# Six more gate blocks as plain matmuls beside the attention, and fewer by seven products, in a decoder layer on one Trainium2 core

## The chip, the cores and the metric

The kernel runs on one core of one Trainium2 chip. The metric is the device time of one launch in microseconds. Engines are named as in the profile: PE is TensorE (PEld its weight loads), DVE VectorE, ACT ScalarE, POOL GpSimd, SP SyncE, which issues nearly all DMAs. SBUF is the on-chip memory, PSUM holds matmul results.

## The reference

One layer of a decoder for 1024 prompt rows and 32 sample rows (1056 columns, as everything is kept transposed), width 1024, all fp32:

```python
h = layer_norm(ALPHA * x + 0.5 * swiglu(x, f1_w1, f1_w3, f1_w2), ln1_g, ln1_b)
z = h @ w_in + b_in               # 42 blocks of 128: 18 for q, k, v; 4 u; 4 v of the spatial gate; 8 ga; 8 gb
# q, k, v: dilated window attention, 3 groups x 4 heads, softmax; groups combined by their denominators
att = combine_groups(outs, lses)
zz = gelu(uv); u, vr = zz[..., :SGU_W], zz[..., SGU_W:]
yb = u * mixed(layer_norm(vr))    # chunks of 128 rows, lower triangular weights
mix = (sigmoid(ga) * (att @ w_oa) + sigmoid(gb) * (yb @ w_ob)) @ w_out
h = layer_norm(ALPHA * h + mix, ln2_g, ln2_b)
h = layer_norm(ALPHA * h + 0.5 * swiglu(h, f2_w1, f2_w3, f2_w2), ln3_g, ln3_b)
```

## The kernel before

Each fp32 matmul is made of three fp32r matmuls (`mm3`, L224): activations and weights are split into a rounded high part (a cast on ACT, L235) and a low part (a subtraction on DVE, L236). The 1056 columns are four chunks of 264.

The stages are `ffn` (first half step), `widen` (the projection z), `mix` (attention, spatial gate, gated products, output projection) and `ffn` again. `widen` computes a block of z in one of two ways. **Plain** (`gate8`): 24 matmuls of 128x128 by 264 columns per chunk, 96 per block; a weight unit is loaded and split (`unit`), ACT evicts with bias and function into a tile M, and a DMA stores it to `zD`. **By seven products** (`pair`): two blocks at once by a Strassen-like scheme, 7 x 24 = 168 matmuls for two, with sums of weights made by `prep` (casts on ACT, sums on POOL, subtractions on DVE). `SPLIT` lists the blocks by seven products in order, `DENSE` the plain ones: 6 at the start (`NLEAD`), the first `CHUNKED` of them chunk by chunk as the normalized chunks come, and `NTAIL` in `mix`.

In `mix` the normalized activations are kept (16 slots) for the last gate blocks. Attention and spatial gate are Python generators in three queues (`bg`, `mid`, `slow`): after each chunk of matmuls `tick(n, m)` runs n steps of `bg`, m of `slow` and 3 of `mid`. `attend(i)` is one of six attention units (head pair, group); L1145 are its scores, L1153 bias and minimum on DVE, L1157 the exponential on ACT, L1168 the transposes, L1184 the products with v, L1206 the last transpose of a unit. After three units `combine` makes the weights of the three groups (DMAs through `mlD` and `cD`), `sample` computes the 32 sample rows on DVE in slabs of keys. Then `local(n)` computes block n of yb @ w_ob, times its gate (`product`, L1491, which evicts the PSUM bank), and a last loop that of att @ w_oa. Bank tags are `mm` (3 buffers) and `ax` (5). SBUF tags are S (37 slots of 4.2 KB a partition), W (8), M (6), R and Q (2 each). A scheduler that simulates the program sets the order on each engine; each engine and each DMA queue then runs its own list in order.

Of the kernel before, what the change touches and what calls it, by code (L numbers as in the profile page):

```python
# [52 lines left out]
HPG = [(hp, g) for hp in range(2) for g in range(3)]  # L53
PAIRS = [HPG[2 * i : 2 * i + 2] for i in range(3)]
URGENT = 300
STEPS = dict(lead=6, strassen=3, seven=2, out=2, tail=5, wob=2, wout=3)
PAUSE = 6
REST = 3
GAP = 4
# [7 lines left out]
QKV = [s * 6 + 2 * g + hp for hp, g in HPG for s in range(3)]  # L67
GATES = [*range(34, 42), *range(26, 34)]
NLEAD = 6
NTAIL = 4  # L70
CHUNKED = 2
SPLIT = [*QKV, 22, 23, 24, 25, 18, 19, 20, 21, *GATES[NLEAD : 16 - NTAIL]]
DENSE = GATES[:NLEAD] + GATES[16 - NTAIL :]
NZ = len(SPLIT) // 2


class Trunk:
# [848 lines left out]
                nc.vector.scalar_tensor_tensor(self.sbias[e, i], p[e], -1.0, mks[e, g], op0=ALU.mult, op1=ALU.add)  # L926
            yield

    def gate8(self, w, nb, c, *steps):
        nc = self.nc  # L930
        p = self.mm_tile()[:, :C]
        self.dense8(p, w, c)
        t = self.M([P, C])
        with self.urgent():
            nc.scalar.activation(t, p, AF.Sigmoid, bias=self.bin(nb))
        nc.sync.dma_start(self.zD[nb][:, c * C : c * C + C], t)
        self.tick(*steps)

# [19 lines left out]
    def pair(self, f, between):  # L958

        nc = self.nc  # L960
        n1, n2 = SPLIT[2 * f], SPLIT[2 * f + 1]
        one, two, three = self.banks()
        ta, tc = self.S([P, NT]), self.S([P, NT])
        gate = n1 >= 26

        def lin(t, nb):
            neg = nb < 6
            return t, nb, self.qb[:, nb : nb + 1] if neg else self.bin(nb), -0.125 if neg else 1.0

        def put(bank, y, e, fn=AF.Identity):  # L970
            t, nb, b, sc = y

            def act(x):
                for o, view in self.parts(t, nb, 2 * x + e):
                    nc.scalar.activation(o, view(bank[x]), fn, bias=b, scale=sc)  # L975
# [20 lines left out]
        def sig(t, x, o, n):  # L996
            c0 = (2 * x + o) * C
            nc.scalar.activation(t[:, c0 : c0 + n * C], t[:, c0 : c0 + n * C], AF.Sigmoid)

        a, c = lin(ta, n1), lin(tc, n2)  # L1000
        go(one, 1, True, put(one, a, 0))
        go(two, 2, True, add(two, a, 0), *([lambda x: sig(ta, x, 0, 1)] if gate else []))
# [3 lines left out]
        go(three, 4, False, add(three, c, 0), *([lambda x: sig(tc, x, 0, 2)] if gate else []))  # L1006
        self.send(tc, n2)
        go(one, 3, False, put(one, a, 1, AF.Sigmoid if gate else AF.Identity))
# [19 lines left out]
    def widen(self):  # L1028
# [22 lines left out]
        for c in range(NC):  # L1051
            self.drain(lns.pop(c))
            if c == NC - 1:
                self.slow.append(self.spread(1, Y, self.A, nc.vector))
            for n in range(CHUNKED):
                self.gate8(units[n], DENSE[n], c, STEPS["lead"], 1)
        units = Y = None
        for n in range(CHUNKED, NLEAD):
            w = self.unit(a["wzp"][n])
            if n == NLEAD - 1:  # L1060
                begin(0)
            for c in (1, 3, 0, 2):
                self.gate8(w, DENSE[n], c, STEPS["lead"], 1)
                if n == NLEAD - 1:
                    next(preps[0], None)
        self.A = None
# [32 lines left out]
    def attend(self, i):  # L1099
# [110 lines left out]
        nc.sync.dma_start(D_.rearrange("m h (i x) -> (m h i) x", x=P), mt)  # L1210
        yield
        if g == 2:
            self.slow.append(self.combine(hp))
            if hp:
                self.slow.append(self.sample_join())

    def combine(self, hp):
# [40 lines left out]
        yield  # L1258
        att = self.S([P, NT])
        self.att[hp] = att  # L1260
        cb = self.S([P, NP])
        for g in range(3):
            for h in range(2):
                nc.sync.dma_start(cb[64 * h : 64 * h + 64], self.cD[hp, g, h].partition_broadcast(64))
            yield
            yield
            aT = self.attT.pop((hp, g))
            if g == 0:
                nc.vector.tensor_tensor(att[:, :NP], aT, cb, op=ALU.mult)
            else:  # L1270
                nc.vector.tensor_tensor(aT, aT, cb, op=ALU.mult)
                nc.vector.tensor_tensor(att[:, :NP], att[:, :NP], aT, op=ALU.add)
            yield

    def sample_rows(self, *blocks):
        nc, a = self.nc, self.a
        yield
        p = self.ax_tile()[:NS, : 2 * P].rearrange("p (s x) -> p s x", s=2)
        for x, (_, t) in enumerate(blocks):
            nc.tensor.transpose(p[:, x], t[:, NP:], self.ident)  # L1280
# [100 lines left out]
    def sgu_norm(self):  # L1381
# [22 lines left out]
        self.swt, self.swb, self.ssb = wt, wb, sb  # L1404
        self.vr = [self.fetch_z(22 + i) for i in range(4)]
        yield from self.pause(4)
        for t in self.vr:
            nc.scalar.activation(t, t, AF.Gelu)
            yield
        vn = [self.S([P, 2, 512]) for _ in range(5)]  # L1410
        mv = self.X([P, 9, 2], "smv", 1)
        nc.vector.memset(mv, 1.0)
# [28 lines left out]
    def sgu_mix(self, gg):  # L1441
# [4 lines left out]
        self.yb[gg] = (hi, lo)  # L1446
        f = slice(gg * P, gg * P + P)
        g = self.cols[:, 90 + gg : 91 + gg]
        nc.scalar.activation(u, u, AF.Gelu)
        yield from self.pause(1)  # L1450
        for b in range(3):
            p = self.ax_tile()
            if b < 2:
# [20 lines left out]
    def mix(self):  # L1474
# [40 lines left out]
        self.drain()  # L1515
        split_att()
        done = 0

# [24 lines left out]
        self.bg.append(sums)  # L1543
        m2 = []
        for n in range(KB):
            wa, ta = self.unit(a["wo"][n], 2 * P), self.fetch_z(26 + n)
            if n < KB // 2:
                local(KB // 2 + n)
            for c in range(NC):
                product(wa, att, c, ta)  # L1550
                self.tick(2)
            nc.vector.tensor_tensor(mt[n], mt[n], ta, op=ALU.add)  # L1552
# [206 lines left out]
```

## Time and profile before

| what | value |
|---|---|
| median of 3 runs | 2310.39 us (2308.38 to 2310.87) |
| profiled execution | 2307.22 us, its span 2305.4 us |
| PE busy | 2164.4 us (94%) |
| DVE, ACT, POOL busy | 1576.9, 935.5, 339.0 us |
| mean granted TensorE clock | 0.964 |

Busy TensorE by slice of 57.6 us, in tenths, and the clock granted to it:

```profile
PE   9999999999998999999898864699999999999997
PEclk9999999999999999999997886899999999999999
```

Read from the left: `ffn` up to slice 12, then `widen` to slice 19, `mix` from slice 19 to 28, `ffn` again. Slices 20 to 25 are those in which TensorE is neither full nor at full clock.

### The profile page before, as it was taken

The numbers are of one execution on the slowest core, as the hardware profiler recorded it, in microseconds if no ns is written. First come the engines' busy times: TensorE is split into PE (matmuls) and PEld (weight loads), VectorE is DVE, ScalarE is ACT, GpSimd is POOL, SyncE is SP. The second block draws the span as 40 slices with busy tenths as digits, with TensorE's granted clock in tenths as the row PEclk, the third lists the DMA queues.
The fourth block names the chain that finished last, engine by engine and source line by source line (L and its number), as shares of the span: only waits on it lengthen the run. The fifth ranks groups of instructions, "written<-read, shape, count | busy, mean of one in ns | idle before, by whom it ended". The sixth has DMA issues, their size and how long they took to land. (4 is left out here: it accounts for less than half of the span.)

```text
span 2305.4 us, 43046 instructions
## 1 busy us (share of the span) xinstructions
PE 2164.4 (94%) x17209; PEld 2107.5 (91%) x17209; DVE 1576.9 (68%) x2722; ACT 935.5 (41%) x1713; POOL 339.0 (15%) x250
## 2 busy tenths in 40 slices
PE   9999999999998999999898864699999999999997
PEld 8999999999988999999876654699999999999997
DVE  8777767566788337878535465658777777746787
ACT  5444444311136333423388830226444344421124
POOL 0423323000000022232000000000323333200000
PEclk9999999999999999999997886899999999999999
DMA  4445454788753246665744334422355454596731
GB/s 159 140 149 187 154 182 168 262 315 295 296 175 117 80 162 218 204 227 196 265 148 137 105 115 134 174 112 96 129 177 180 159 181 158 186 347 253 274 141 76
DMA packets 161048, 416.83 MB, mean 181 GB/s; under 512 B 23808, under 2 KB 57328, under 8 KB 158160
## 3 DMA queue, kind: packets, MB, share of 16 engines
q1 hardware_dynamic: 160416, 413.55, 51.0%
q8 instruction: 135, 2.21, 0.4%
q14 instruction: 65, 0.53, 0.1%
q10 hardware_dynamic: 432, 0.54, 0.1%
HBM read 301.64 MB, written 158.57 MB: 200 GB/s over the span
## 5 line engine op out<-in xcount | busy, mean ns | idle before, releaser
L224 PE MATMUL ax<-S,W 128*128 128x264 f32 x5688 | 743.0, 284 | 0.6 <-ACT S L975 0.6
L224 PEld LDWEIGHTS ax<-S,W 128*128 128x128 f32 x5688 | 712.7, 188 | 2.3 <-ACT S L975 1.2
L224 PE MATMUL mm<-S,W 128*128 128x264 f32 x4632 | 638.7, 294 | 72.1 <-DVE S L1491 59.1
L224 PEld LDWEIGHTS mm<-S,W 128*128 128x128 f32 x4632 | 605.6, 196 | 84.8 <-DVE S L1491 61.2
L224 PE MATMUL ax<-S,S 128*128 128x264 f32 x3432 | 505.4, 285 | 0.5 <-DVE S L984 0.5
L224 PEld LDWEIGHTS ax<-S,S 128*128 128x128 f32 x3432 | 453.6, 188 | 1.9 <-DVE S L984 0.7
L224 PE MATMUL mm<-S,S 128*128 128x264 f32 x2472 | 390.8, 286 | 14.1 <-ACT S L235 9.5
L224 PEld LDWEIGHTS mm<-S,S 128*128 128x128 f32 x2472 | 337.3, 189 | 16.5 <-ACT S L235 10.0
L235 ACT CAST W<-R 128x1024 fp32r<-128x1024 f32 (+3 forms) x170 | 125.8, 756 | 427.0 <-PE mm L224 195.8
L366 POOL TENSOR_TENSOR Q<-R 128x512 f32<-128x512 f32 x53 | 73.8, 1392 | 847.2 <-DMA R<-w13a 237.4
L235 ACT CAST W<-Q 128x1024 fp32r<-128x1024 f32 (+1 forms) x82 | 80.9, 987 | 233.5 <-POOL Q L367 127.7
L236 DVE TENSOR_TENSOR W<-R,W 128x1024 fp32r<-128x1024 f32 (+3 forms) x170 | 148.1, 878 | 20.7 <-ACT W L235 20.6
L778 DVE SCALAR_TENSOR_TENSOR S<-ax,S 128x264 f32<-128x264 f32 x240 | 98.9, 426 | 58.0 <-PE ax L224 57.4
L441 DVE TENSOR_TENSOR S<-ax,M 128x264 f32<-128x264 f32 x84 | 33.5, 432 | 151.9 <-PE ax L224 151.9
L236 DVE TENSOR_TENSOR S<-Q,S 128x1024 fp32r<-128x1024 f32 (+2 forms) x90 | 127.7, 1419 | 7.1 <-ACT S L235 6.3
L235 ACT CAST S<-Q 128x1024 fp32r<-128x1024 f32 (+2 forms) x90 | 89.5, 994 | 100.6 <-PE ax L224 72.0
L103 POOL CAST S<-ones 128x1 fp32r<-128x1 f32 x32 | 13.5, 444 | 785.5 <-DVE S L1552 382.0
L236 DVE TENSOR_TENSOR W<-Q,W 128x1024 fp32r<-128x1024 f32 (+1 forms) x82 | 94.8, 1156 | 41.1 <-ACT W L235 41.0
L367 POOL TENSOR_TENSOR Q<-Q,R 128x512 f32<-128x512 f32 x53 | 87.6, 1652 | 2.7
L236 DVE TENSOR_TENSOR S<-S,M 128x528 fp32r<-128x528 f32 x72 | 85.3, 1185 | 2.5 <-ACT M L235 0.9
L374 POOL TENSOR_TENSOR Q<-R,Q 128x512 f32<-128x512 f32 x53 | 86.5, 1633 | 1.4
L372 POOL TENSOR_TENSOR Q<-R,R 128x512 f32<-128x512 f32 x53 | 80.7, 1523 | 20.7 <-ACT M L437 13.5
(200 smaller groups left out, 2089.2 us busy)
## 6 DMA issues: line engine op xcount, KB each, us to landing
ws<-st SPq DMA_DIRECT2D x144, 256.0 KB
S<-sumsA SPq DMA_DIRECT2D x63, 528.0 KB
S<-sumsB SPq DMA_DIRECT2D x63, 528.0 KB
M<-kv SPq DMA_DIRECT2D x96, 256.0 KB
sumsA<-M SPq DMA_DIRECT2D x90, 264.0 KB
sumsB<-M SPq DMA_DIRECT2D x90, 264.0 KB
R<-w13b SPq DMA_DIRECT2D x44, 512.0 KB
S<-zD SPq DMA_DIRECT2D x42, 528.0 KB
```

Source lines behind the costliest of these rows:

```text
L103: self.nc.gpsimd.tensor_copy(t[:, 0, :1] if len(shape) == 3 else t[:, :1], self.ones[:, :1])
L224: mm = lambda a, b, s, e: nc.tensor.matmul(o, a[:, cc], b, start=s, stop=e, skip_group_check=True)
L235: a = self.nc.scalar.copy(hi, src)
L236: b = self.nc.vector.tensor_tensor(lo, src, hi.bitcast(F32), op=ALU.subtract)
L366: tt(s12[:, lo], cd[:, lo], cd[:, hi], op=ALU.add)
L367: tt(s12[:, hi], s12[:, lo], ab[:, lo], op=ALU.subtract)
L372: tt(s34[:, lo], ab[:, lo], cd[:, lo], op=ALU.subtract)
L374: tt(s34[:, hi], ab[:, hi], s12[:, hi], op=ALU.subtract)
L441: go(one, 5, False, lambda x: tt(h[:, x, 1], one[x], p7[:, x], op=ALU.add))
L778: nc.vector.scalar_tensor_tensor(y(x, r, e), bank[x], HALF, y(x, r, e), op0=ALU.mult, op1=ALU.add)
```

## The change

- 26 instead of 32 blocks of z go by seven products (13 pairs instead of 16); the six are gates, and become plain blocks in `mix`: `NTAIL` is 10 instead of 4. The first six of the ten go block by block, the last four chunk by chunk. Per chunk 3 instead of 5 steps of `bg` run.
- Gates in `mix` are stored with bias but without Sigmoid; the Sigmoid is applied to the whole loaded block just before its products.
- The Gelu of u and v is applied in `pair` as the blocks are evicted, instead of after loading in the spatial gate.
- Loads of gates for the products stand two blocks ahead. `combine` runs in `mid` instead of `slow`, with three buffers for the group weights instead of one. `sample_rows` waits four steps instead of one.
- Three instead of two lead blocks go chunk by chunk (`CHUNKED`).

```diff
-STEPS = dict(lead=6, strassen=3, seven=2, out=2, tail=5, wob=2, wout=3)
+STEPS = dict(lead=6, strassen=3, seven=2, out=2, tail=3, wob=2, wout=3)
-NTAIL = 4
-CHUNKED = 2
+NTAIL = 10
+LAST = 4
+CHUNKED = 3
+LATE_GATES = DENSE[NLEAD:]
...
-    def gate8(self, w, nb, c, *steps):
+    def gate8(self, w, nb, c, fn, *steps):
...
-            nc.scalar.activation(t, p, AF.Sigmoid, bias=self.bin(nb))
+            nc.scalar.activation(t, p, fn, bias=self.bin(nb))
...
-        gate = n1 >= 26
+        fn = None if n1 < 18 else AF.Gelu if n1 < 26 else AF.Sigmoid
...
-            self.slow.append(self.combine(hp))
+            self.mid.append(self.combine(hp))
...
-        cb = self.S([P, NP])
-        for g in range(3):
+        cbs = [self.S([P, NP]) for _ in range(3)]
+        for g, cb in enumerate(cbs):
             for h in range(2):
                 nc.sync.dma_start(cb[64 * h : 64 * h + 64], self.cD[hp, g, h].partition_broadcast(64))
-            yield
-            yield
+        yield from self.pause(3)
+        for g, cb in enumerate(cbs):
             aT = self.attT.pop((hp, g))
...
-        yield
+        yield from self.pause(4)
         p = self.ax_tile()[:NS, : 2 * P].rearrange("p (s x) -> p s x", s=2)
...
-        for t in self.vr:
-            nc.scalar.activation(t, t, AF.Gelu)
-            yield
...
-        nc.scalar.activation(u, u, AF.Gelu)
-        yield from self.pause(1)
...
-            mt[n] = self.fetch_z(34 + n)
+            if n + 2 < KB:
+                mt[n + 2] = self.fetch_z(36 + n)
+            if 34 + n in LATE_GATES:
+                nc.scalar.activation(mt[n], mt[n], AF.Sigmoid)
...
-        units = [self.unit(a["wzp"][NLEAD + n]) for n in range(NTAIL)]
+        for n in range(NLEAD, NLEAD + NTAIL - LAST):
+            w = self.unit(a["wzp"][n])
+            for c in (0, 2, 1, 3):
+                self.gate8(w, DENSE[n], c, AF.Identity, STEPS["tail"], 1)
+        units = {n: self.unit(a["wzp"][n]) for n in range(NLEAD + NTAIL - LAST, NLEAD + NTAIL)}
         for c in range(NC):
-            for n in range(NTAIL):
-                self.gate8(units[n], DENSE[NLEAD + n], c, STEPS["tail"], 1)
+            for n in units:
+                self.gate8(units[n], DENSE[n], c, AF.Identity, STEPS["tail"], 1)
         units = self.A = None
+        for n in range(2):
+            mt[n] = self.fetch_z(34 + n)
...
-        self.drain()
+        ta = [self.fetch_z(26 + n) for n in range(2)]
+        while self.bg or self.mid or self.slow:
+            self.tick(1, 1)
...
-            wa, ta = self.unit(a["wo"][n], 2 * P), self.fetch_z(26 + n)
+            wa = self.unit(a["wo"][n], 2 * P)
+            if n + 2 < KB:
+                ta.append(self.fetch_z(28 + n))
             if n < KB // 2:
                 local(KB // 2 + n)
+            if 26 + n in LATE_GATES:
+                nc.scalar.activation(ta[n], ta[n], AF.Sigmoid)
             for c in range(NC):
-                product(wa, att, c, ta)
+                product(wa, att, c, ta[n])
```

Lines after L70 move by 2 to 13 in the changed kernel: L224 becomes L226, L935 L937, L1157 L1159, L1206 L1208, L1264 L1266, L1491 L1488.

How the lists of the engines change, at three places. First ACT at the start of `mix`, in the first attention unit. L935 (L937) is the eviction of a gate chunk, L1157 (L1159) the exponential, L1172 (L1174) the copy of transposed probabilities. Before:

```order
L1172 COPY S_13529<-ax_13521 128x2x128
L1172 COPY S_13529<-ax_13522 128x512
L935 ACTIVATE M_13777<-mm_13752,cols 128x264
L1157 ACT_TABLE_LOAD
L1157 ACTIVATE S_13532,X_13460<-S_13532,X_13460 128x256 x4
L935 ACT_TABLE_LOAD
L935 ACTIVATE M_13877<-mm_13852,cols 128x264
L1172 COPY S_13564<-ax_13554 128x512
L1172 COPY S_13564<-ax_13555 128x512
L1157 ACT_TABLE_LOAD
L1157 ACTIVATE S_13567,X_13460<-S_13567,X_13460 128x256 x4
```

Now:

```order
L1174 COPY S_12815<-ax_12808 128x512
L1159 ACTIVATE S_12818,X_12758<-S_12818,X_12758 128x256 x3
L937 ACTIVATE M_13103<-mm_13078,cols 128x264
L1174 COPY S_12850<-ax_12840 128x512
L1174 COPY S_12850<-ax_12841 128x512
L1159 ACTIVATE S_12853,X_12758<-S_12853,X_12758 128x256 x4
L937 ACTIVATE M_13172<-mm_13147,cols 128x264
```

The loads of a function table between exponential and gate eviction are gone.

Second PE, in an attention unit of the third group (before) and of the second group (now). L1145 (L1147) are scores, L1168 (L1170) transposes, L1184 (L1186) products with v, L224 (L226) with a tile mm a gate block. Before:

```order
L1184 MATMUL ax_14221<-S_14203,Q_14108 64x128 x4
L1168 MATMUL ax_14226<-ident,S_14206 128x128
L1168 MATMUL ax_14227<-ident,S_14206 128x128
L1145 MATMUL ax_14236<-S_13736,S_13734 128x128 x2
L1145 MATMUL ax_14237<-S_13736,S_13734 128x128 x2
L1168 MATMUL ax_14226<-ident,S_14206 128x128
L1168 MATMUL ax_14227<-ident,S_14206 128x128
L1184 MATMUL ax_14221<-S_14232,Q_14108 64x128 x4
```

Now:

```order
L1186 MATMUL ax_13327<-S_13342,Q_13181 64x128 x4
L226 MATMUL mm_13675<-S_8222,W_13581 128x264
L226 MATMUL mm_13675<-S_8224,W_13581 128x264
L226 MATMUL mm_13675<-S_8222,W_13582 128x264
L1170 MATMUL ax_13401<-ident,S_13345 128x128
L1170 MATMUL ax_13402<-ident,S_13345 128x128 x2
L1147 MATMUL ax_13413<-S_12694,S_12692 128x128
L1147 MATMUL ax_13413<-S_12694,S_12692 128x256
```

The last three of a gate chunk's 24 matmuls stand here between products and transposes, the other 21 ahead of the products; before, the units of the third group ran with none beside them.

Third SP, at the end of the attention. L1264 (L1266) loads the group weights, which L1257 (L1259) stored; L1083 (L1085) loads a block of z. S_14994 and S_15120 are the gates of `local(0)` and `local(1)` before, S_15320 and S_15322 now. Before:

```order
L1083 DMA S_14955<-zD 128x1056
L1083 DMA S_14994<-zD 128x1056
L1083 DMA S_15120<-zD 128x1056
L1357 DMA M_15528<-jD 64x66 x4
L1210 DMA mlD<-X_15075 32x128
L1117 DMA M_15078<-bD 64x64
```

Now:

```order
L938 DMA zD<-M_15313 128x264
L1359 DMA M_15366<-jD 64x66 x4
L209 DMA ws<-st 16x4096
L1259 DMA cD<-S_15109 16x128 x3
L1266 DMA S_15142<-cD 64x1024 x2
L1266 DMA S_15143<-cD 64x1024 x2
L1266 DMA S_15144<-cD 64x1024 x2
L1085 DMA S_15320<-zD 128x1056
L1085 DMA S_15322<-zD 128x1056
L1085 DMA S_15331<-zD 128x1056
```

The loads of the first gates stand behind the last weights' loads now; before they stood ahead of both head pairs' combinations.

More of the change, by code (lines that the diff above doesn't have):

```diff
@@ L994, in go, with bend @@
             between()
-        def sig(t, x, o, n):
+        def bend(t, x, o, n):
             c0 = (2 * x + o) * C
-            nc.scalar.activation(t[:, c0 : c0 + n * C], t[:, c0 : c0 + n * C], AF.Sigmoid)
+            nc.scalar.activation(t[:, c0 : c0 + n * C], t[:, c0 : c0 + n * C], fn)
         a, c = lin(ta, n1), lin(tc, n2)
         go(one, 1, True, put(one, a, 0))
-        go(two, 2, True, add(two, a, 0), *([lambda x: sig(ta, x, 0, 1)] if gate else []))
+        go(two, 2, True, add(two, a, 0), *([lambda x: bend(ta, x, 0, 1)] if fn else []))
         go(one, 6, False, put(one, c, 0))
@@ L1005, in pair @@
         go(one, 5, False, add(one, c, 1))
-        go(three, 4, False, add(three, c, 0), *([lambda x: sig(tc, x, 0, 2)] if gate else []))
+        go(three, 4, False, add(three, c, 0), *([lambda x: bend(tc, x, 0, 2)] if fn else []))
         self.send(tc, n2)
-        go(one, 3, False, put(one, a, 1, AF.Sigmoid if gate else AF.Identity))
+        go(one, 3, False, put(one, a, 1, fn or AF.Identity))
         self.send(ta, n1)
@@ L1055, in widen @@
             for n in range(CHUNKED):
-                self.gate8(units[n], DENSE[n], c, STEPS["lead"], 1)
+                self.gate8(units[n], DENSE[n], c, AF.Sigmoid, STEPS["lead"], 1)
         units = Y = None
@@ L1062, in widen @@
             for c in (1, 3, 0, 2):
-                self.gate8(w, DENSE[n], c, STEPS["lead"], 1)
+                self.gate8(w, DENSE[n], c, AF.Sigmoid, STEPS["lead"], 1)
                 if n == NLEAD - 1:
@@ L1545, in mix @@
         for n in range(KB):
-            wa, ta = self.unit(a["wo"][n], 2 * P), self.fetch_z(26 + n)
+            wa = self.unit(a["wo"][n], 2 * P)
+            if n + 2 < KB:
+                ta.append(self.fetch_z(28 + n))
             if n < KB // 2:
                 local(KB // 2 + n)
+            if 26 + n in LATE_GATES:
+                nc.scalar.activation(ta[n], ta[n], AF.Sigmoid)
             for c in range(NC):
-                product(wa, att, c, ta)
+                product(wa, att, c, ta[n])
                 self.tick(2)
-            nc.vector.tensor_tensor(mt[n], mt[n], ta, op=ALU.add)
+            nc.vector.tensor_tensor(mt[n], mt[n], ta[n], op=ALU.add)
             m2.append((self.S([P, NT], F32R), self.S([P, NT], F32R)))
```

## The prediction

> **What bounds the kernel now.** I read the times by stage first, to see where TensorE is not solid. The columns are: stretch in us, its length, then busy time and instruction count of PE, PEld, DVE, ACT and POOL, the granted TensorE clock, the DMA share and GB/s.
>
> ```profile
> 816.00:1080.00 264.00, 257.58 (x2096) 255.83 (x2095) 193.27 (x312) 97.20 (x189) 67.80 (x48) 0.99 0.60 205
> 1142.50:1351.60 209.10, 175.50 (x1223) 136.03 (x1223) 95.32 (x350) 160.99 (x362) 0.00 (x0) 0.86 0.40 135
> 1351.60:1401.00 49.40, 15.60 (x107) 14.56 (x105) 25.55 (x54) 5.83 (x11) 0.00 (x0) 0.69 0.47 139
> 1401.00:1498.00 97.00, 66.63 (x421) 64.70 (x422) 60.98 (x92) 17.42 (x21) 3.65 (x10) 0.79 0.46 159
> ```
>
> The block pairs (first row) keep TensorE busy at full clock: there only fewer matmuls save time. The other three rows are `mix` up to its output projection: attention, the hole after it, and the gated products. TensorE is granted 0.69 to 0.86 of its clock there and is idle for long spans. Who it waits for says why (total us, times, longest):
>
> ```profile
> PE mm L224 <- DVE S L1491: 59.1, 9, 24.4
> PE ax L1168 <- ACT S L1157: 18.8, 8, 6.7
> PE ax L1125 <- DMA S<-zD: 6.2, 1, 6.2
> PE ax L1184 <- ACT S L1172: 3.2, 6, 0.9
> ```
>
> L1491 is the product with a gate; it frees the PSUM bank that the next matmul group needs. DVE itself waits there for the gate's load:
>
> ```profile
> DVE S L1491 <- DMA S<-zD: 24.2, 6, 7.3
> ```
>
> So three things bound `mix`: ScalarE's exponentials in the attention, the combination of the heads (the 24.4 us hole), and gates that are loaded too late.
>
> **The change, part by part.** The profiled execution took 2307.22 us for a span of 2305.4; the median of the runs is 2310.39, 3.2 us more. I sum against 2307.2 and add the 3.2 at the end.
>
> *Three block pairs fewer.* The price of one matmul is that of a solid stretch, 23.20/190 = 0.1221 us:
>
> ```profile
> 752.02 23.20 PE L224 MATMUL mm<-S,W 128*128 128x264 f32 x190
> ```
>
> A pair is 7 products of 24 matmuls, 168 x 0.1221 = 20.5 us. The stores of finished pairs agree: from pair 12's last to pair 15's last are 63.25 us for three, 21.1 each.
>
> ```profile
> 1079.01 0.38 SPq L1017 DMA_DIRECT2D zD<-S  x1
> 1142.26 0.56 SPq L1017 DMA_DIRECT2D zD<-S  x1
> ```
>
> Three pairs go: **-61.5 us**, between -60 and -63. The Gelu that now bends four pairs takes the place of the Sigmoid in the three dropped ones; ACT is busy 97 of 264 us there, so it is hidden at nothing. If that cover were gone, it would be some four activations of half a us, 2 us a pair.
>
> *Sample rows two steps later.* TensorE waits at this transpose:
>
> ```profile
> PE ax L1280 <- ACT S L975: 5.4, 4, 2.6
> ```
>
> With four steps instead of one the evictions are long done: **-4 us** (0 to -5.4).
>
> *Three instead of two lead blocks by chunk.* TensorE runs out of work there before the last normalized chunk is ready:
>
> ```profile
> 732.19 0.51 PE L224 MATMUL mm<-S,S 128*128 128x264 f32 x2 [0.71 <-ACT S L235]
> 733.55 2.94 PE L224 MATMUL mm<-S,S 128*128 128x264 f32 x22 [0.86 <-DVE S L236]
> 741.26 0.81 PE L224 MATMUL mm<-S,S 128*128 128x264 f32 x2 [4.78 <-ACT S L235]
> ```
>
> That is 6.35 us of idle time. Three chunks more per normalized chunk, and a first part of pair 0's matmuls that now stands among them, are 2.9 us each: **-5 us** (0 to -8, if the slow clock behind the hole goes too). The two extra slots might delay something; I take no loss, since the load there is issued at low urgency.
>
> *Ten instead of four gate blocks in the attention.* The old stretch runs from the last pair's end, 55 gate matmuls ahead of 1142.5 (so about 1135.7), to the last attention unit's transpose L1206 at 1351.60: 216 us. In it are 384 matmuls of four gate blocks and about 132 of `local`, 516 x 0.1221 = 63 us. What the attention and the spatial gate themselves need on TensorE, I take from the same stretch with L224 alone:
>
> ```profile
> 1142.50:1351.60 209.10, 70.17 (x456) 61.75 (x455) 0.86 0.40 135
> ```
>
> The rest is 175.50 - 70.17 = 105.3 us of PE, or 136.03 - 61.75 = 74.3 of PEld, at clock 0.86: at full clock between 64 (74.3 x 0.86) and 91. I take the middle, 78. So 216 - 63 - 78 = 75 us were waits and slow clock. In the changed order the last transpose stands 22 matmuls before the end of the 40th gate chunk: 938 x 0.1221 = 114.5 us of gates, no `local`, and 78, so 192.5 us. Of the waits I keep the 6.2 us for the first q, k, v load (the same 62 or so matmuls stand ahead of it), a third of the 22 us of L1168 and L1184, 7, since a gate chunk now stands beside most softmax steps, and 12 us for the clock: 25. The stretch is then 217.5, **+2 us**. Bounds: 199 if only the load's wait stays (-17), and 114.5 + (216 - 63) = 267.5 if gates and attention don't overlap at all (+51).
>
> ScalarE is what lets me cut the waits to a third. It was busy 161 of 209 us, and switched tables at each change between exponential and Sigmoid:
>
> ```profile
> L1157 ACT ACT_TABLE_LOAD x16 | 20.5, 1283 | 0.3
> L935 ACT ACT_TABLE_LOAD x13 | 16.7, 1283 | 1.5 <-issue 1.3
> 1156.70 0.48 ACT L935 ACTIVATE M<-mm,cols 128x264 f32<-128x264 f32 x1 [5.37 <-DMA zD<-M]
> 1157.20 1.28 ACT L1157 ACT_TABLE_LOAD   x1
> 1158.50 0.40 ACT L1157 ACTIVATE S<-S,X 128x128 f32<-128x128 f32 x1
> L1408 ACT ACTIVATE S<-S 128x1056 f32<-128x1056 f32 x4 | 4.4, 1092 | 0.0
> ```
>
> With gates stored through Identity, nearly all of these 29 loads go (37 us), and the eight Gelus of 1.09 us with them; 24 evictions of 0.48 us and six weight casts of about 1 us come: some 28 us less on ACT in a stretch as long as before. The load costs 1.28 us and the next instruction follows at once, here 0.02 us later.
>
> The Trainium skill, "ScalarE: Activation LUTs", section "What ACT_TABLE_LOAD costs", adds a drain of about 1.38 us to each switch. The rows above show none of it: the load starts as the ACTIVATE before it ends. By that rule the 29 loads would have held ScalarE another 40 us, it would have been the stretch's limit at 201 of 209 us, and the sum would have the 7 us of waits gone too, so 7 us lower than mine.
>
> *Gates loaded ahead, ten Sigmoids late, heads combined earlier.* From the last transpose to the output projection the old kernel needs 146.2 us, 1351.60 to 1497.81:
>
> ```profile
> 1351.60 0.27 PE L1206 MATMUL ax<-ident,X 128*32 128x128 f32 x1
> 1358.12 14.23 PE L224 MATMUL mm<-S,W 128*128 128x264 f32 x96 [5.45 <-DVE S L1491]
> 1401.10 10.73 PE L224 MATMUL mm<-S,W 128*128 128x264 f32 x72 [24.39 <-DVE S L1491]
> 1497.81 2.45 PE L224 MATMUL mm<-S,W 128*128 128x264 f32 x18 [1.01 <-DVE S L1569]
> ```
>
> In the new order SyncE issues the first gate loads only behind the six loads of the combining weights, and these wait for the weights to be written. Old rows price that:
>
> ```profile
> 1361.11 0.52 SPq L1210 DMA_DIRECT2D mlD<-X  x1
> 1378.14 1.27 SPq L1257 DMA_DIRECT2D cD<-S  x3
> 1379.54 12.77 SPq L1264 DMA_DIRECT2D S<-cD  x6
> 1392.35 1.06 SPq L1083 DMA_DIRECT2D S<-zD  x2
> ```
>
> From the store of the maxima to that of the weights are 17 us. New: 2 us from the transpose to the store, 17, 1.4 to the first load, six issues of 0.5 us with three buffers instead of one wait after another, and about 7 for three loads to land and three products: DVE reaches the first product with a gate about 31 us after the transpose. TensorE has 22 gate matmuls and three `local` chunks of 12 until its three banks are full, 7 us: a **hole of 24 us remains**, as long as the old one. Behind it come 17 chunks of 12 (24.9 us), so the attention's own projection starts after 56 us (old: 51). Then the gates lie ready, and DVE is the limit: it was busy 60.98 of the last 97 us. I take 64 for this part (the Sigmoids, 10 x 1.09, lie beside it on an ACT busy 17 of 97). Sum 120 against 146: **-26 us**. Bounds: no hole at all, 7 + 25 + 60 = 92, -54; and the last part as long as ever, 31 + 25 + 91 = 147, about 0.
>
> Sum: -61.5 - 4 - 5 + 2 - 26 = -94.5, so 2212.7 by the profiled execution, and **2216 us** beside the median.
>
> **The rivals.**
> First, attention stays serial: PSUM and slots are shared, and in-order TensorE waits at each step with the gates bunched. For it: 16 of 37 slots stay taken by the normalized activations until the gates end, and in the new order six gate chunks stand without any attention between two units. Against it: most steps do have gates beside them. Then +51 in place of +2: 2265.
> Second, the tail gives nothing back (DVE and ACT wait on each other in their queues): 0 in place of -26, 2242.
> Third, the overlap is nearly full: the stretch takes 205 (-11) and the tail 110 (-36): 2193.
> Fourth, slower: the gate evictions starve for the six mid-size buffers. Three are held by the sample's key slabs and one or two by the bias, and each gate's store queues on SyncE behind slab loads that wait for DVE. ScalarE then stands at the eviction, and the exponentials behind it. The trace has seen it:
>
> ```profile
> ACT M L935 <- DMA zD<-M: 6.5, 2, 5.4
> ```
>
> Two waits in 16 chunks are 0.4 us a chunk. If each of the 24 added chunks cost 5.4 us, that is +130: 2346, slower. It decides from 94.5/24 = 3.9 us a chunk, ten times what is seen.
>
> **How the numbers follow.** My forecast has 0.53, the full overlap 0.14, the tail that gives nothing 0.13, serial attention 0.12, starved buffers 0.06; 0.02 is for no change. Faster by over 0.2% (about 4.6 us, what a measurement of this kernel can tell from no change) is 0.53 + 0.14 + 0.13 + 0.12 = 0.92, same 0.02, slower 0.06. The range goes from just under the full overlap, 2180, to nearly the serial case, 2262; it leaves out the slower case, half of the serial one, and what lies past the lower bounds.
>
> **What would show it.** Right: about 61 us less between the first pair and the last; no table loads at the gate evictions; last transpose of the attention about 217 us after the last pair; one TensorE wait of 20 to 25 us behind it on L1488, the gate product's new line; gated products in some 64 us with no wait for zD. Wrong: waits of evictions for zD stores, exponential waits over 20 us in sum, or a stretch of over 240 us.

## The result, and the profile after

The changed kernel takes **2224.06 us** (median of 4 runs, 2220.93 to 2227.92); the kernel before, beside it, 2309.74 us (2308.38 to 2310.87). The ratio of the two is 0.963, with a 95% interval of [0.961, 0.965]: 3.7% faster. The profiled execution took 2226.7 us, its span is 2224.9 us. The forecast was 2216, within 2180 to 2262.

To see where the time went I cut both programs at four points: the last store of the first block pair, that of the last pair, the last transpose of the attention, and the first matmul after the output projection (L528 before, L530 after). These are rows of the timeline (start and length in us, engine, line). Those of before that were not shown yet:

```profile
817.09 0.32 SPq L1017 DMA_DIRECT2D zD<-S  x1
1526.06 0.61 PE L528 MATMUL ax<-M,ones 128*128 128x264 f32 x2
```

and all four of after:

```profile
806.62 0.32 SPq L1019 DMA_DIRECT2D zD<-S  x1
1065.27 0.32 SPq L1019 DMA_DIRECT2D zD<-S  x1
1296.23 0.27 PE L1208 MATMUL ax<-ident,X 128*32 128x128 f32 x1
1441.39 0.61 PE L530 MATMUL ax<-M,ones 128*128 128x264 f32 x2
```

| part, us | before | after | difference | forecast |
|---|---|---|---|---|
| start to first pair's end | 817.09 | 806.62 | -10.5 | -5 |
| pairs | 325.17 | 258.65 | -66.5 | -65.5 |
| attention, to its last transpose | 209.34 | 230.96 | +21.6 | +2 |
| rest of `mix` | 174.46 | 145.16 | -29.3 | -26 |
| layer norm and second half step | 779.3 | 783.5 | +4.2 | 0 |
| span | 2305.4 | 2224.9 | -80.5 | -94.5 |

The sum misses by 14 us. The attention alone is 19.6 us over, and the last part 4.2; the lead stage gave 5.5 more than forecast, the rest of `mix` 3.3 and the pairs 1. Beside the medians the miss is only 8 us, since the profiled execution lies 2.6 us over the median here, and the one before lay 3 us under it.

By slice of 55.6 us, the page after shows what is left of TensorE's weak part, in slices 20, 24 and 28 counted from 1 (before, counted the same way, it was slices 20 and 22 to 26):

```profile
PE   9999999999999999999899979998999999999997
```

The lead stage (columns as in the prediction: PE, PEld, DVE, ACT and POOL busy, clock, DMA share, GB/s), first before, then after, over the same 115 us:

```profile
634.00:749.00 115.00, 102.23 (x790) 99.84 (x789) 100.82 (x163) 61.39 (x101) 5.42 (x16) 0.96 0.41 147
634.00:749.00 115.00, 110.71 (x883) 109.04 (x882) 103.24 (x167) 64.06 (x106) 6.96 (x16) 0.99 0.44 155
```

TensorE gets 93 more matmuls done in it. The attention after, all instructions, then the matmuls of L226 alone (here: the gate blocks):

```profile
1064.00:1296.30 232.30, 218.36 (x1656) 184.33 (x1654) 127.11 (x391) 123.02 (x345) 0.00 (x0) 0.97 0.51 165
1064.00:1296.30 232.30, 130.31 (x888) 116.18 (x886) 0.97 0.51 165
```

TensorE is busy for 218 of 232 us, at clock 0.97 instead of 0.86: little is left to fill. ACT is at 123 instead of 161 us. The two longest sums of TensorE's waits from the last pair to 1352, which is beyond the attention's end:

```profile
PE mm L226 <- DVE S L1488: 15.1, 2, 14.9
PE mm L226 <- ACT M L937: 6.1, 3, 3.7
```

The 18.8 us of waits for exponentials are gone; so are the loads of function tables between them and the evictions (before: 16 and 15 in the whole program):

```profile
L937 ACT ACT_TABLE_LOAD x2 | 2.6, 1283 | 0.0
L1159 ACT ACT_TABLE_LOAD x2 | 2.6, 1283 | 0.0
```

The hole behind the attention is 14.89 us, and its chain is on SP: maxima out, weights out, weights in, gates in.

```profile
1319.58 5.60 PE L226 MATMUL mm<-S,W 128*128 128x264 f32 x29 [14.89 <-DVE S L1488]
1296.84 0.31 SPq L1212 DMA_DIRECT2D mlD<-X  x1
1306.45 1.26 SPq L1259 DMA_DIRECT2D cD<-S  x3
1308.44 3.66 SPq L1266 DMA_DIRECT2D S<-cD  x6
1312.14 5.93 SPq L1085 DMA_DIRECT2D S<-zD  x8
```

### The profile page after: what moved, and what is told of

The parts are those of the page before. It is cut to its first block, busy times and chain, and to the rows that moved or that the text cites. A ratio compares the mean times of both kernels' runs of the same rounds, so it can differ in the third digit from the quotient of the medians.

```text
span 2224.9 us, 43158 instructions
## 1 busy us (share of the span) xinstructions
PE 2156.3 (97%) x17281; PEld 2104.8 (95%) x17281; DVE 1559.7 (70%) x2698; ACT 898.8 (40%) x1684; POOL 330.8 (15%) x238
## 4 chain that ended last, share of the span: by engine, by line
PE 82%; DMA 6%; DVE 6%; ACT 2%; issue 2%; POOL 1%; SPq 1%; ACTq 0%; DVEq 0%; POOLq 0%
PE ax L226 43%; PE mm L226 35%; DMA M<-kv 2%; PE ax L1147 1%; DVE W L238 1%; DVE S L238 1%; PE ax L1170 1%; PE ax L1186 1%; DMA R<-wz 1%; DMA zD<-M 1%; DMA S<-zD 1%; DMA zD<-S 0%; DVE S L604 0%; DVE S L1488 0%; DVE M L1328 0%
## 5 line engine op out<-in xcount | busy, mean ns | idle before, releaser
L226 PE MATMUL mm<-S,W 128*128 128x264 f32 x5040 | 685.3, 291 | 38.4 <-DVE S L1488 23.0
L226 PE MATMUL ax<-S,W 128*128 128x264 f32 x5472 | 716.9, 285 | 0.3 <-ACT S L977 0.2
L226 PEld LDWEIGHTS mm<-S,W 128*128 128x128 f32 x5040 | 647.4, 193 | 55.4 <-DVE S L1488 19.6
L226 PEld LDWEIGHTS ax<-S,W 128*128 128x128 f32 x5472 | 685.5, 188 | 2.7 <-ACT S L977 1.3
L226 PE MATMUL ax<-S,S 128*128 128x264 f32 x3288 | 484.8, 285 | 1.6 <-DVE S L986 1.4
L226 PEld LDWEIGHTS ax<-S,S 128*128 128x128 f32 x3288 | 434.5, 188 | 3.5 <-DVE S L986 2.5
L226 PE MATMUL mm<-S,S 128*128 128x264 f32 x2496 | 391.7, 287 | 5.8 <-ACT S L237 3.3
L226 PEld LDWEIGHTS mm<-S,S 128*128 128x128 f32 x2496 | 341.0, 190 | 7.4 <-ACT S L237 3.5
L237 ACT CAST W<-R 128x256 fp32r<-128x256 f32 (+2 forms) x172 | 127.9, 759 | 369.7 <-PE mm L226 134.6
L238 DVE TENSOR_TENSOR W<-R,W 128x256 fp32r<-128x256 f32 (+2 forms) x172 | 148.4, 870 | 28.2 <-ACT W L237 27.8
L105 POOL CAST S<-ones 128x1 fp32r<-128x1 f32 x32 | 19.2, 625 | 769.8 <-DVE S L238 613.5
L237 ACT CAST S<-R 128x512 fp32r<-128x512 f32 (+1 forms) x65 | 44.4, 686 | 91.5 <-DMA sumsA<-S 37.9
```

The lines of the kernel that those rows point to most:

```text
L105: self.nc.gpsimd.tensor_copy(t[:, 0, :1] if len(shape) == 3 else t[:, :1], self.ones[:, :1])
L226: mm = lambda a, b, s, e: nc.tensor.matmul(o, a[:, cc], b, start=s, stop=e, skip_group_check=True)
L237: a = self.nc.scalar.copy(hi, src)
L238: b = self.nc.vector.tensor_tensor(lo, src, hi.bitcast(F32), op=ALU.subtract)
```

## The experiments

Each edit is against the changed kernel unless said otherwise. Ten of the kernels have the same code for the 13 pairs; yet from the first zD store of the pairs to the last it took them 257.9 to 265.6 us. So a difference of a few us between two profiles is not given a cause here. The kernel before ran again beside every experiment, with medians of 2310.2 to 2313.3 us; so a difference in medians and one in ratios are not quite the same, and both are given where it matters.

**The six blocks back to the pairs.** 4 instead of 10 plain blocks in `mix`, with 5 attention steps a chunk as before.

```diff
-tail=3, NTAIL = 10
+tail=5, NTAIL = 4
```

> The changed kernel with the move of the six blocks alone undone: 16 pairs again, 4 plain gate blocks beside the attention at 5 steps per chunk; late Sigmoid, Gelu in the pairs, gates ahead, combination and lead blocks as changed. Theory A (the move pays, because attention alone waits on its own chain): three pairs come back, +61.5 us, and the attention stretch falls only from 238 to about 200 us, so about 2248 us. Rival B (the move pays nothing, all comes from what ScalarE no longer does and from the tail): the stretch falls by the six blocks' 70 us, so about 2215 us.

2236.78 us, ratio 0.968 [0.9664, 0.9697], against 0.963: about 12 us slower, between the two theories. Its pairs last 62.6 us longer (from the first store to the last, 324.2 against 261.6), its attention 29.0 less (202.0), the rest of `mix` 24.7 less (120.5). Attention, all instructions and L226 alone, and TensorE's longest wait, now for a split behind the attention:

```profile
1127.00:1329.00 202.00, 178.69 (x1333) 145.58 (x1331) 107.09 (x377) 111.11 (x323) 0.00 (x0) 0.91 0.49 161
1127.00:1329.00 202.00, 87.58 (x569) 77.31 (x567) 0.91 0.49 161
PE mm L226 <- DVE S L238: 14.9, 2, 14.6
```

The six blocks by seven products cost 62.6 us, plain 576 x 0.1221 = 70 us. They only pay by what they fill. From the last pair's last store to the end of `mix`, first in this kernel, then in the changed one:

```profile
1127.40:1450.00 322.60, 269.66 (x1995) 232.69 (x1994) 192.92 (x515) 141.10 (x359) 7.90 (x10) 0.88 0.52 174
1065.30:1441.40 376.10, 338.51 (x2555) 300.90 (x2554) 224.71 (x563) 165.72 (x397) 7.82 (x10) 0.95 0.55 182
```

TensorE is idle for 52.9 us in the first and 37.6 in the second: the plain blocks filled some 15 us. So the move that gives the change its name is worth some 12 us of 86 by the medians (9.5 by the two profiled spans); the other edits, without it, already give 73.

**Gates and attention one after the other.** No attention steps beside the gate chunks (`tail=0`).

> The changed kernel with no step of the attention queue beside the ten gate blocks, so that attention runs after the gates, beside the local products. Theory A (overlap of gates and attention is worth some 50 us): about 2280 us; the 40 gate chunks take 117 us, and attention after them waits on exponentials again. Rival C (interleaving itself slows the gate matmuls, 0.147 us each in the changed kernel against 0.122 alone, so the overlap is worth little): about 2240 us. The attention's own TensorE time, without gate or local matmuls, is about 88 us by theory A (as in the changed kernel) and under 78 if interleaving had swollen it.

2251.89 us, ratio 0.9743 [0.972, 0.9766]: the overlap is worth 28 us, nearer to theory C. The attention's stretch is 287.2 us instead of 231.0, but what follows it is 23.8 shorter, since 295 more matmuls, of the local products, already ran in it (1183 against 888). By the rows the attention's own share is 256.15 - 156.85 = 99.3 us, which neither theory had (88, or under 78); the account of the attention below says why the rows can't tell. All instructions, then L226 alone:

```profile
1064.00:1352.00 288.00, 256.15 (x1950) 219.29 (x1949) 143.23 (x431) 132.35 (x358) 0.00 (x0) 0.91 0.51 166
1064.00:1352.00 288.00, 156.85 (x1183) 148.53 (x1181) 0.91 0.51 166
```

**Sigmoid at the eviction again.** `gate8` in `mix` with Sigmoid, none after loading.

```diff
-LATE_GATES = DENSE[NLEAD:]
+LATE_GATES = []
-self.gate8(..., AF.Identity, STEPS["tail"], 1)
+self.gate8(..., AF.Sigmoid, STEPS["tail"], 1)
```

> The changed kernel with Sigmoid applied again as the gates in the attention are evicted, none after loading. Theory D (table loads on ScalarE would bound the stretch with 40 gate chunks in it): 60 to 80 loads of 1.28 us more, ScalarE busy 200 us or more of the stretch, and 15 to 30 us longer: 2240 to 2255 us. Rival E (ScalarE is off the path since TensorE is full): within 5 us of 2224.

2239.16 us, ratio 0.9685 [0.9663, 0.9707]: 13 us (by the ratios) to 15 us slower, theory D, though with fewer loads and less of ACT's time than it had. The table loads are back (in the stretch), ACT is busy 189 us, and TensorE waits for the evictions (and 4.7 us for exponentials):

```profile
L937 ACT ACT_TABLE_LOAD x26 | 33.4, 1283 | 9.8 <-DMA zD<-M 8.1 <-DVE M L1436 0.9 <-PE mm L226 0.2
L1159 ACT ACT_TABLE_LOAD x24 | 30.8, 1283 | 0.6 <-DVE X L1155 0.2
1067.00:1311.30 244.30, 223.55 (x1672) 188.48 (x1671) 128.41 (x392) 188.78 (x397) 0.00 (x0) 0.96 0.48 158
PE mm L226 <- ACT M L937: 10.4, 4, 6.6
```

The 50 loads take 64 us of ACT, and the attention's stretch gets 11.6 us longer (242.6 against 231.0): ACT, at 189 of 244 us, has room for most of them.

**Gates loaded late.** Each gate's load right before its products instead of two blocks ahead, in both halves.

> The changed kernel with each gate loaded just before its products, as before, all else kept. Theory F (the loads ahead are what shortens the gated products): their part grows by about 25 us, with waits of DVE for zD as before, about 2250 us. Rival G (DVE work bounds that part anyway and the loads are mostly hidden): about 2230 us.

2255.74 us, ratio 0.9763 [0.9743, 0.9782]: 32 us slower, the largest of the single parts; theory F. What DVE's products wait for, and one of TensorE's five waits of 5 to 7 us behind the hole:

```profile
DVE S L1488 <- ACT S L1494: 9.9, 2, 5.3
1376.41 10.84 PE L226 MATMUL mm<-S,W 128*128 128x264 f32 x72 [7.00 <-DVE S L1488]
```

L1494 is the late Sigmoid of the local half; for that of the other half, L1556, DVE waits another 8.5 us: when the load is late, the Sigmoid stands between it and the product as well.

**Two lead blocks by chunk.** `CHUNKED = 2`.

> CHUNKED = 2 in place of 3, the rest as in the changed kernel: how much of the lead stage's gain of 10.5 us (pair 0's last zD store 817.09 before, 806.62 after) is the third chunked block. Theory G (the third block's matmuls fill the 6.35 us of waits at 732 to 741 and give the weights of the next block time to arrive): the wait comes back, pair 0's last store lands at 812 to 817, and the time is 5 to 10 us over the changed kernel's, 2229 to 2234. Theory H (the lead gain comes from elsewhere, from the order of the rows of the samples or from the Gelu that left): within 2 us of the changed kernel, 2222 to 2226.

2233.85 us, ratio 0.9652 [0.9633, 0.9672]: slower by 5 (by the ratios, whose intervals overlap) to 10 us (by the medians), theory G. The first pair ends at 816.52, as before the change, and TensorE waits again for the normalized activations, here for the seventh of their eight casts:

```profile
739.95 1.07 ACT L237 CAST S<-S 128x1056 fp32r<-128x1056 f32 x1
741.07 0.81 PE L226 MATMUL mm<-S,S 128*128 128x264 f32 x2 [4.75 <-ACT S L237]
```

That the third block also gives the next weights time to arrive, as theory G has it, is not shown.

**The combination in its old form.** In the slow queue, one buffer.

```diff
-self.mid.append(self.combine(hp))
+self.slow.append(self.combine(hp))
...
-cbs = [self.S([P, NP]) for _ in range(3)]  # six loads, pause(3)
+cb = self.S([P, NP])                       # two loads, two steps, three times
```

> The combination of the heads goes back to the old form: in the slow queue, and with one buffer for the broadcast weights, two steps a load; all else as in the changed kernel. Theory P (the earlier combination is what shortened the chain from the maxima's store to the weights' store from 17 us to 9.6, and the three buffers let the gate loads pass): the chain takes 15 us or more again, the six cD loads 12 us instead of 3.7, the wait for the first gated products grows from 14.9 to 25 us or more, 2234 to 2245. Theory Q (the chain is shorter only because ScalarE and DVE are less busy there): the hole stays at 15 to 18 us, 2222 to 2229.

2239.72 us, ratio 0.9687 [0.9666, 0.9708]: 13 us (by the ratios) to 16 us slower, within theory P's range, but not by its path. The attention ends 21 us sooner after the last pair (1277.41 - 1067.58 = 209.8), but the rest of `mix` takes 33 us longer. The combination of the second head pair now comes 32 us behind that of the first, and the gates pass it; TensorE waits instead at the sample's transpose and at the attention's own projection, 32 us in three waits:

```profile
1307.30 1.26 SPq L1259 DMA_DIRECT2D cD<-S  x3
1339.41 1.26 SPq L1259 DMA_DIRECT2D cD<-S  x3
1337.59 0.47 PE L1378 MATMUL ax<-ident,X 128*128 128x128 f32 x1 [10.58 <-DVE X L1375]
1348.45 1.69 PE L226 MATMUL mm<-S,W 128*128 128x264 f32 x6 [9.72 <-DVE S L238]
1361.63 1.03 PE L226 MATMUL mm<-S,W 128*128 128x264 f32 x3 [11.49 <-ACT S L237]
```

**Sample rows one step later, as before.** `pause(1)` in `sample_rows`.

> The transposes of the sample's rows wait one step again instead of four; all else as in the changed kernel. The prediction put 4 us on this edit in nine pairs (six pairs of q, k and v). Theory R (TensorE waited for the activation that the transpose reads): the waits at L1282 come back with some 4 us in the pairs, 2227 to 2229. Theory S (the waits are made up later in a pair, or the new place of the Gelu changed them): within 2 us of 2224.

2226.75 us, by the median between the two theories; the ratio, 0.9632 [0.961, 0.9655], is the changed kernel's. The waits come back (0.8 us in the changed kernel), but its pairs last 260.6 us against 261.6:

```profile
PE ax L1282 <- ACT S L977: 6.7, 3, 2.6
```

Theory S, as far as this can be told: 4 us are within what the same pairs differ by from kernel to kernel.

**Two gates loaded ahead of the last combination.** The first loads of the tail go two rounds of gate chunks earlier.

```diff
         for c in range(NC):
+            if c == NC - 2:
+                mt[:2] = [self.fetch_z(34 + n) for n in range(2)]
             for n in units:
...
-        for n in range(2):
-            mt[n] = self.fetch_z(34 + n)
```

> The first two gate loads of the tail (blocks 34 and 35) are issued ahead of the last two rounds of chunks of the last four gate blocks, so they stand on SP ahead of the cD loads and the last combine. Theory J (the hole of 14.9 us before the first gated products of the local half is the time of the mlD store, cD round trip and the gate loads queued behind them on SP): the hole shrinks to between 0 and 7 us, and the time falls by 8 to 15 us to 2209 to 2216. Theory K (the first products wait for the combine or for DVE, whatever the loads do, and what is freed there is waited for at the next gate): the hole stays at 12 us or turns up at the following products, and the time is within 4 us of the changed kernel's 2224.

**2210.05 us** (2207.31 to 2210.94), ratio 0.9549 [0.9532, 0.9566]: theory J, and the fastest kernel of this study. It beats the changed kernel by 14 us in the medians; the intervals of the two ratios lie apart. The hole is 6.7 us, and from the last transpose (1292.96) to the end of `mix` (1427.32) it takes 134.4 us instead of 145.2:

```profile
1319.76 5.65 PE L226 MATMUL mm<-S,W 128*128 128x264 f32 x24 [6.71 <-DVE S L1488]
```

**Attention in fewer gate chunks.** `tail=6` instead of 3: it ends early, and the last 540 matmuls before the products, nearly all of gates, run by themselves over the combination.

> The attention is drained at 6 in place of 3 steps a gate chunk: its PE instructions are spread over some 390 gate matmuls with 64 changes between gate and attention instead of 870 with 160, and the last gate chunks then run by themselves and cover the last combine. Theory L (mixing costs PE: a gate matmul among attention is charged 0.147 us, by itself 0.120; 24 us over 160 changes are 0.15 us each): 96 changes fewer save some 14 us, the hole of 14.9 us is covered, the waits for the exponentials come back with some 15 us: about 2210, PE's busy time from the last pair to the first gated product falls by 10 us or more. Theory M (PE's time for the attention and the gates is the same however they are mixed; only waits count): busy time the same within 5 us, the hole of 15 is exchanged for 15 to 20 us of exponential waits, 2222 to 2232. Theory N (attention at this rate is latency-bound, as it was before at 5 steps): waits of 30 us or more, slower than 2232.

2215.7 us, ratio 0.957 [0.9549, 0.9592]: 8 us faster than the changed kernel, between theories L and M. The hole is covered, and the waits for exponentials are 11.5 us. But as M said, the mix makes no difference to TensorE's own time. This kernel, all and L226 alone, and its wait for exponentials; then the one with gates loaded ahead over the same work:

```profile
1064.00:1325.00 261.00, 239.10 (x1842) 204.35 (x1841) 145.66 (x426) 135.94 (x362) 0.00 (x0) 0.93 0.56 181
1064.00:1325.00 261.00, 139.35 (x1066) 132.13 (x1065) 0.93 0.56 181
PE ax L1170 <- ACT S L1159: 11.5, 6, 5.9
1064.00:1323.00 259.00, 242.29 (x1846) 207.78 (x1845) 146.79 (x431) 128.78 (x356) 0.00 (x0) 0.97 0.54 172
1064.00:1323.00 259.00, 152.67 (x1070) 138.00 (x1069) 0.97 0.54 172
```

1842 instructions in 239.1 us, 1846 in 242.3, though the rows charge a gate matmul 0.131 us in the one and 0.143 in the other. The charge moves with the mix; the sum does not.

**Both of these together.**

> Both edits that shortened the hole: 6 steps of the attention a gate chunk, and the two gates loaded ahead. Theory V (both remove the same wait, since TensorE has 540 matmuls in one piece behind the attention in the first, and so nothing is left to gain from loading ahead): within 4 us of the better of the two, 2207 to 2216. Theory W (the 10.5 us of short waits for L1488 that the first still has are waits for gate loads as well): 5 us or more under 2210.

2219.43 us, ratio 0.9597 [0.9573, 0.962]: no gain, so not theory W, and 3 us above what V allowed. Its profiled span is 10.5 us over that of the kernel with 6 steps, whose profiled run was its fastest, 6.4 us under its median; 5.7 of the 10.5 are there before the last pair's last store, in code that both share. The rest stays open.

**Sums of the halves on GpSimd**, in the 2210 us kernel.

```diff
-nc.vector.tensor_tensor(mt[n], mt[n], ta[n], op=ALU.add)
+nc.gpsimd.tensor_tensor(mt[n], mt[n], ta[n], op=ALU.add)
```

> The kernel with the two gates loaded ahead of the last combination (2210.05 us), and in it the eight sums of the two halves (128x1056, 1.25 us each on DVE) on GpSimd. Theory T (the last 57 us of gated products are DVE's: 55.75 of 57.6 busy): DVE has 10 us less, the part gets 5 to 9 us shorter, 2201 to 2206. Theory U (the sum lies in the chain to the next split, and GpSimd takes some 3.3 us for it by its 1.54 us for 128x512; or it slows DVE): 0 to 5 us longer, 2209 to 2215.

2214.29 us, ratio 0.9572 [0.9546, 0.9598]: some 4 us slower, though the two intervals overlap; in any case no gain, theory U. Two of the eight sums on POOL, and DVE beside them:

```profile
1374.09 1.31 DVE L1546 SCALAR_TENSOR_TENSOR S<-S,X,S 128x1056 f32<-128x1056 f32 x1
1374.30 3.40 POOL L1564 TENSOR_TENSOR S<-S,S 128x1056 f32<-128x1056 f32 x1 [1.43 <-DVE S L1488]
1382.33 3.28 POOL L1564 TENSOR_TENSOR S<-S,S 128x1056 f32<-128x1056 f32 x1 [4.63 <-issue]
1375.32 0.42 DVE L1488 TENSOR_TENSOR S<-S,mm 128x264 f32<-128x264 f32 x1
1375.66 3.12 DVE L238 TENSOR_TENSOR W<-R,W 128x1024 fp32r<-128x1024 f32 x1
1383.26 3.47 DVE L238 TENSOR_TENSOR S<-S,S 128x1056 fp32r<-128x1056 f32 x1
1382.12 1.21 DVE L238 TENSOR_TENSOR W<-R,W 128x1024 fp32r<-128x1024 f32 x1
```

In the order of the fence: a DVE instruction with two inputs in SBUF that runs when the first sum starts; two sums on POOL; a product that reads PSUM; two subtractions of splits that start during the sums, and one that doesn't. The two end 1.1 us after POOL's sum does; the product keeps its 0.42 us.

**Column sums of the output weights ahead**, in the 2210 us kernel: five loads and reductions moved from the gated products to the local ones.

> The kernel with the two gates loaded ahead of the last combination (2210.05 us; ratio 0.9549), and in it the column sums of the output weights (five loads, five reductions of 1.21 us and two small ones on DVE) stand before the local products, beside the last combination, instead of among the gated products of the attention half. Theory X (those 57 us are DVE's, 55.75 busy, and GpSimd brought nothing only because it takes 2.96 us a sum and slows DVE's splits meanwhile): 6.5 us leave that part, TensorE waits less there, 3 to 6 us gained, ratio 0.952 to 0.9535. Theory Y (DVE's load there comes on top of a chain split, product, sum that has its own length; or the reductions now delay the combination): within 2 us of 2210 or slower, ratio 0.954 to 0.957.

2213.58 us (5 runs), ratio 0.9568 [0.955, 0.9586]: theory Y. DVE is busy 52.0 instead of 55.75 of 57.6 us in the part that was to gain, but the hole grows by 1.5 us (from 6.71 to 8.24), and from the last transpose to the end of `mix` it takes 134.1 us, as without the edit (134.4). That part without the edit, then with it:

```profile
1337.00:1394.60 57.60, 50.64 (x369) 48.48 (x368) 55.75 (x87) 22.25 (x26) 7.63 (x9) 0.91 0.61 203
1339.00:1396.60 57.60, 51.69 (x381) 49.96 (x381) 52.00 (x84) 23.65 (x28) 6.49 (x9) 0.91 0.57 188
```

Not tried: a kernel with more than six M buffers, and the Gelu alone.

## Why the prediction was right, and where not

**The pairs: right.** -66.5 against -61.5 - 4. A pair's share of the pairs' time before is 325.17/15 = 21.7 us, not 20.5: three are 65. So the whole difference is three pairs, and the 4 us for the sample's rows (three steps later, not two as its heading has it), a term of its own, were not there: undoing that edit alone brought its waits back but no time that could be measured.

**The lead stage: right place, half the size.** -10.5 against -5. The forecast took the idle time between 732 and 741, 6.35 us; without the third chunked block the first pair's end came back by 9.9 us. The bound of -8 was too narrow.

**The attention: the step that failed.** Forecast 217.5 us from the last pair's end, measured 238 (1058.26 to 1296.23). The term that was mis-sized is "what the attention and the spatial gate themselves need on TensorE": 78, from PE's 105.3 and PEld's 74.3 us *scaled by the clock of 0.86*, bounds 64 to 91. Taking the gate matmuls off TensorE's whole busy time at 0.1221 us each, as they run by themselves, leaves for the rest:

| kernel | PE busy - gate matmuls x 0.1221, us | clock |
|---|---|---|
| before | 175.50 - 456 x 0.1221 = 119.8 | 0.86 |
| six blocks in the pairs | 178.69 - 569 x 0.1221 = 109.2 | 0.91 |
| one after the other | 256.15 - 1183 x 0.1221 = 111.7 | 0.91 |
| 6 steps a chunk | 239.10 - 1066 x 0.1221 = 108.9 | 0.93 |
| Sigmoid at the eviction | 223.55 - 904 x 0.1221 = 113.2 | 0.96 |
| the change | 218.36 - 888 x 0.1221 = 109.9 | 0.97 |
| gates loaded ahead | 242.29 - 1070 x 0.1221 = 111.6 | 0.97 |

For the same 764 to 776 instructions it is 109 to 113 us at any mix and any clock from 0.91 to 0.97, 32 over the forecast. Two errors made the 78. The row of L224 alone charges a gate matmul among small ones 0.154 us instead of 0.1221, so the 105.3 were 15 too few. Most of that is not the slow clock, since the changed kernel's row charges 130.31/888 = 0.147 at 0.97. And taking them to 78 by the clock, and by PEld's smaller time, took off 27, where from 0.86 to 0.97 the busy time fell by 10: 78 + 15 + 27 - 10 = 110. Whether the clock made those 10 is open. Against that, the waits came to 14 us instead of the forecast 25: those for the exponentials went wholly, and no 12 us had to be added for the clock. With 114 us of gates, as forecast, 110 and 14 make the 238.

So rival 1 (serial attention) was wrong as a mechanism: the two do overlap, and with no attention step beside the gate chunks the kernel takes 28 us more. What stood against the gain is that TensorE is full. Rival 4's mechanism is there at the size that was seen before: ACT waits for M buffers that the stores to zD still read, 13.8 us in 40 chunks, 0.35 us a chunk, a tenth of the 3.9 from which it would have decided; TensorE waited 6.1 us for evictions in all. Such waits were one of the forecast's signs of being wrong; they decided nothing here.

```profile
ACT M L937 <- DMA zD<-M: 13.8, 5, 6.5
```

**ScalarE: right, and more of it.** 28 us less was forecast, 161 - 123 = 38 measured: 34 table loads are gone from the stretch where the forecast counted 29, those beside the Gelus among them. Putting the Sigmoids back costs 13 to 15 us. The Trainium skill's rule that the prediction quoted ("ScalarE: Activation LUTs", "What ACT_TABLE_LOAD costs": a drain of about 1.38 us a switch) does not hold here: ACT was busy 189 us with the 50 loads, and 50 drains, 69 us, would have taken it past the 244 us that there were.

**The tail: right by two errors.** -29.3 against -26. The hole was forecast at 24 us, since the chain from the maxima's store to the weights' store was priced at the old 17 us; it took 9.6 (1296.84 to 1306.45), and the hole 14.9. The gated products took 58 us from the sample's transpose at 1347.00 to the last of them, against the forecast 64, with no wait of DVE for zD:

```profile
1347.00:1405.00 58.00, 49.28 (x342) 46.77 (x341) 53.52 (x90) 22.76 (x27) 3.91 (x7) 0.89 0.59 195
```

But the forecast set its 120 us against an old 146.2 that runs to 1497.81, some 9 us into the output projection; like for like, the old part ends with the last gated product at 1488.8 and lasts 137, the new one 108. What the hole gave more, this took back.

**DVE as the limit of the gated products: half right.** DVE is busy 53.5 of those 58 us, but taking 3.75 us off it moved the wait instead of ending it.

**The end: not foreseen.** The last part is 4.2 us longer, with the same code. In the twelve kernels of the experiments, with the same code again, it takes 779.8 to 784.5 us, so 783.5 lies in that spread; the cause is open.

## What to carry to other kernels

Work that is moved under idle time is worth at most that idle time: here 70 us of plain matmuls took the place of 62.6 us in pairs and filled some 15 us of idle TensorE, 10 to 12 us net, while four edits to who waits for whom (gates loaded ahead, combination earlier, no switch of function tables, a third lead block) cost 5 to 32 us each when undone one by one. To price mixed work on TensorE, take the busy time of the whole stretch and subtract the part with a known price; in these profiles neither the rows' split between small and large instructions nor scaling by the granted clock gave it. And a load that stands behind another chain in an in-order DMA queue inherits that chain's waits: moving two issues ahead of it was worth 14 us, as much as the six blocks or more.

## What the runs showed of the hardware

A subtraction on DVE with both inputs in SBUF that starts while GpSimd runs a sum does not run beside it: at 1375.66 it took 3.12 us instead of 1.21, and ended 1.08 us after GpSimd's at 1377.70. A product on DVE with one input in PSUM is not held: one at 1342.12, inside GpSimd's sum from 1341.82 to 1344.29, took 0.43 us as always. The Trainium skill, "GPSIMD Engine Reference", section "1. Specifications", lists GpSimd's SBUF interfaces as shared with VectorE, with contention for DVE instructions that have two SBUF inputs; these rows agree.

It holds the other way as well. Of the eight sums of 128x1056, the two that started with no such DVE instruction running took 2.47 and 2.45 us. The other six started during one and took 2.54 to 3.41 us, each ending 2.3 us after that instruction did (the first in the fence: 1377.70 against 1375.40). DVE takes 1.25 us for such a sum.
